# State space part of a hybrid decoder layer: packed array tiles for its tables and its output, shared PSUM banks, one table load

## The chip, the cores and the metric

The kernel runs on one core of one Trainium2 chip. The core has a matmul engine (PE, TensorE), a vector engine (DVE), a scalar engine (ACT) and a general engine (POOL), each with a queue of its own that it works off in order; SP issues most DMAs. Matmuls write to PSUM, eight banks of 512 f32 columns by 128 partitions; everything else lies in SBUF or in DRAM. The metric is the time of one execution in microseconds, as the device measures it. The time before is 2601.95 us, the median of three runs.

## The reference

One layer for one sequence of 2048 tokens, width 1024. Its input projection feeds two groups: forgetting attention with 8 heads of 64, and a state space group with 32 groups of 16 channels and 64 complex states each. Both outputs are normalised and go through one output projection; a gated MLP with a short convolution follows. The change touches the state space group alone:

```python
def s5_ssm(u, a_re, a_im, log_dt, b_re, b_im, c_re, c_im, d_skip, w_glu, b_glu):
    lam = lax.complex(a_re, a_im)
    dt = jnp.exp(log_dt)[:, None]
    lam_bar = jnp.exp(lam * dt)
    b_bar = ((lam_bar - 1.0) / lam)[:, :, None] * b_mat
    bu = jnp.einsum('bsgc,gpc->bsgp', ug, b_bar)
    _, h = lax.associative_scan(_scan_op, (a, bu), axis=1)
    y = jnp.real(jnp.einsum('bsgp,gcp->bsgc', h, c_mat)) + d_skip * ug
    z = jax.nn.gelu(y)
    gate = jnp.einsum('bsgc,gcd->bsgd', z, w_glu) + b_glu
    out = z * jax.nn.sigmoid(gate)
```

## The kernel before, in words

The 2048 tokens are 256 chunks of 8, and the 32 groups are 16 pairs, so that a pair has 2 x 64 states on the 128 partitions, and 2 x (8 x 16) inputs of a chunk. Within a chunk the inputs act on the outputs directly through a block Toeplitz matrix (128 x 128 for each group, `tt_d`); between chunks a state is carried.

`ssm_tables` prepares, in four batches of four pairs, all that depends on the parameters alone, and writes it to DRAM: `tab_d` (for each pair 1024 columns: 256 that bring the inputs into the state, 512 of cosines and sines, 256 that bring the state into the outputs) and `tt_d`. For `tt_d` there are products of 16 x 128 (L785, L786), 64 in all, each of 64 rows; DVE copies them into the tile `kz` (L787) and adds D on the diagonal; eight shifted DMAs for each half (L795) lay `kz` out as the Toeplitz matrix. `wb` (L800 to L802) is the transposed input table.

`ssm` then runs over the 16 pairs. `stage_a` of pair p loads the tables, transposes the inputs (`in_ps`, L838), forms the inputs of the state (`ss_ps`, L846: four products of 64 output rows), and on DVE turns them by cosine and sine, scans over the 256 chunks (L857) and turns them back to `hs` (L851 to L864). `stage_b` of pair p - 1 forms y (`y_ps`, L872 to L874: for each group one product with `ttg` and two with `ft`, in which the other group's 64 rows are zero), the GELU with two ACT and two DVE instructions (L877 to L881, result `z`), the gate product (`g_ps`, L886), its tanh (L889), their product on DVE (L892), four transposes (`tr_ps`, L897) and two copies to `vout` (L900). `y_ps` has a bank of its own; `g_ps` and `tr_ps` share a second one by turns; `in_ps` and `ss_ps` share a third. A bank comes free when its last reader is done. The `ft` tiles are zeroed once, and two DMAs a pair fill their halves (L822). After each fourth pair the outputs go to DRAM (L926), and `mix_t` reads them back as `row` (L1194), takes the squares, scales the rows (L1202), transposes them (L1206) and hands them to the output projection (L1232).

The functions record what is to be done; a scheduler interleaves this into one order for each engine, by its own estimate of when each buffer and operand is ready. The state space part is recorded with high priority. What it leaves free is filled by what is recorded behind it and is ready: attention of block 0 (L952 to L1054), and the query, key and value products of blocks 2 and 3 (L470 and L437, 24 matmuls for each result); when these are done, attention of block 1. DVE does the lower halves, sums and maxima of the attention (L956, L959, L1009, L1017) and the vectors `ada_mid` (L1113) in the same queue as the state space part.

The lines of the change stand one to four lower in its own numbering: there the y products are L871 and L875, the gate product L886, the output transposes L894 (all on `y_ps`), the inputs L837 and L845, the query, key and value products L470 and L437 as before, and attention L948 to L1050.

Of the kernel before, what the change touches and what calls it, by code (L numbers as in the profile page):

```python
# [12 lines left out]
F32 = mybir.dt.float32  # L13
# [3 lines left out]
AF = mybir.ActivationFunctionType  # L17
ALU = mybir.AluOpType
AX = mybir.AxisListType
# [3 lines left out]
P = 128  # L23
# [6 lines left out]
NG = 32  # L30
NPAIR = NG // 2
# [89 lines left out]
def hybrid_layer(ctx, tc, x, c_t, w_ada, b_col, gains, w_flat, bf_row, a_re, a_im, log_dt,  # L121
# [526 lines left out]
    def ssm_tables(pp):  # L648
        misc_ps = prep_ps
# [14 lines left out]
        Q.dma_start(ci, sc_im)  # L664
        ds_t = tl("ds", [16, NG])
        Q.dma_start(ds_t, dskip)

# [38 lines left out]
        V.tensor_tensor(out=fi, in0=fi, in1=den, op=ALU.mult)  # L706
        bbr, bbi, t16 = tl("bbr", [P, NPAIR, 16]), tl("bbi", [P, NPAIR, 16]), tl("t16", [P, NPAIR, 16])
        b3 = [P, NPAIR, 16]
# [34 lines left out]
        def batches(marks):  # L743


            kz = tl("kz", [16, 4, 16, 16])
            G.memset(kz[:, :, 0:8, :], 0.0)
            kt = kz[:, :, 8:16, :]
            for q in range(4):
                with tc.issue_after(marks[q].ins):  # L750
# [28 lines left out]

                    for half in range(2):  # L780
                        ps = misc_ps()
                        rs = slice(half * 64, half * 64 + 64)
                        for pr in range(4):
                            po = ps[0:16, pr * P : (pr + 1) * P]
                            T.matmul(po, lhsT=bbr[rs, 4 * q + pr, :], rhs=f_re[rs, pr, 0:8, :], start=True, stop=False)  # L785
                            T.matmul(po, lhsT=bbi[rs, 4 * q + pr, :], rhs=f_im[rs, pr, 0:8, :], start=False, stop=True)  # L786
                        V.tensor_copy(kt, ps[0:16, :].rearrange("c (g m d) -> c g m d", g=4, m=8))  # L787
                        dg = tl("dg", [16, 4, 16])
                        dsq = ds_t.rearrange("c (q p h) -> c q h p", q=4, h=2)[:, q, half, :]
                        V.tensor_tensor(out=dg, in0=ident[0:16, 0:16].unsqueeze(1).broadcast_to([16, 4, 16]),  # L790
                                        in1=dsq.unsqueeze(2).broadcast_to([16, 4, 16]), op=ALU.mult)
                        V.tensor_tensor(out=kt[:, :, 0, :], in0=kt[:, :, 0, :], in1=dg, op=ALU.add)
                        dst = tt_d[q].rearrange("(p h) k n -> h k p n", h=2)[half]
                        for j in range(8):
                            Q.dma_start(dst[j * 16 : (j + 1) * 16], kz[:, :, 8 - j : 16 - j, :].rearrange("c g m d -> c g (m d)"))  # L795
                    for pr in range(4):
                        wb = tl("wb", [P, 2 * P])
                        ps = misc_ps()
# [11 lines left out]
    def ssm(sp, sps):  # L810

        fts = [sp.tile([P, 2, 2, P], F32, name=f"ft{i}", bufs=1) for i in range(2)]
        for ft in fts:
            G.memset(ft, 0.0)
# [52 lines left out]
        def stage_b(p, vout, ft, ttg, glt, ug, hs):  # L867

            yp = sps.tile([P, 512], F32, name="y_ps", tag="y", bufs=1)
            for g in range(2):  # L870
                yo = yp[:, g * 256 : (g + 1) * 256]  # L871
                T.matmul(yo, lhsT=ttg[:, g, :], rhs=ug[:, g, :], start=True, stop=False)  # L872
                T.matmul(yo, lhsT=ft[:, 0, g], rhs=hs[:, 0, 0:256], start=False, stop=False)
                T.matmul(yo, lhsT=ft[:, 1, g], rhs=hs[:, 1, 0:256], start=False, stop=True)  # L874

            y2 = sp.tile([P, 512], F32, name="y2", tag="y2", bufs=1)
            A.activation(y2, yp, AF.Square, scale=math.sqrt(0.044715))  # L877
            V.scalar_tensor_tensor(out=y2, in0=y2, scalar=1.0, in1=yp, op0=ALU.add, op1=ALU.mult)
            A.activation(y2, y2, AF.Tanh, scale=math.sqrt(2.0 / math.pi))
            z = sp.tile([P, 512], F32, name="z", tag="z")  # L880
# [3 lines left out]
            th = sp.tile([P, 512], F32, name="th", tag="th")  # L884
            for g in range(2):
                T.matmul(gp[:, g * 256 : (g + 1) * 256], lhsT=glt[:, g, :], rhs=z[:, g * 256 : (g + 1) * 256],  # L886
                         start=True, stop=True)
            for g in range(2):
                A.activation(th[:, g * 256 : (g + 1) * 256], gp[:, g * 256 : (g + 1) * 256], AF.Tanh, scale=0.25,  # L889
                             bias=hb[:, 2 * p + g : 2 * p + g + 1])  # L890
            o4 = th
            V.scalar_tensor_tensor(out=o4, in0=th, scalar=1.0, in1=z, op0=ALU.add, op1=ALU.mult)  # L892
            c0 = (p % 4) * 32
            pt = sps.tile([P, 512], F32, name="tr_ps", tag="out", bufs=1)  # L894
            for kb in range(2):
                for g in range(2):
                    T.transpose(pt[:, (2 * kb + g) * P : (2 * kb + g + 1) * P],  # L897
                                o4[:, g * 256 + kb * P : g * 256 + (kb + 1) * P], ident)
            for kb in range(2):
                A.activation(vout[kb][:, :, c0 : c0 + 32].rearrange("k t (g c) -> k g t c", g=2),  # L900
                             pt[:, kb * 256 : (kb + 1) * 256].rearrange("k (g t c) -> k g t c", g=2, t=8), AF.Copy, scale=0.25)

# [1024 lines left out]
```

## Time and profile before

| | |
|---|---|
| three runs | 2596.57, 2601.95, 2602.49 us |
| profiled execution | 2602.08 us, of which the span 2600.4 us |
| instructions | 35785 |
| mean granted clock of PE | 0.98 |
| HBM | 374.32 MB read, 139.59 MB written |

The span runs from the first instruction to the last. A busy share is the mean over stages with different limits; the chain of waits tells which engine's work ended last. Matmuls are pipelined, so that one row of PE can begin before the one ahead of it has ended: the distance between two starts is what a matmul costs, not its length. An f32 product is two records of PE. The state space part stands between 348.7 us (first input transpose) and 573.0 us (last output transposes).

### The profile page before, as it was taken

To read this page: it belongs to the slowest core of one execution; us is meant where nothing else is said; L and a number is where in the kernel's file an instruction comes from. 1 tells how busy PE (TensorE), PEld (TensorE's weight loads), DVE (VectorE), ACT (ScalarE), POOL (GpSimd) and SP (SyncE) were. 2 spreads that over 40 slices of the span, in tenths; PEclk is the share of its full clock that TensorE was granted. 3 is DMA by queue.
4 is the path that set the end of the run, shared out by engine and by line. 5 is a ranking of instruction groups with operands and counts; after the bars stand their busy time and mean duration, and the time that the engine had idled before them with its cause. 6 is when DMAs were issued, how large, how long until landed. Compare 5 with 4: busy or idle time off the path is not lost.

```text
span 2600.4 us, 35785 instructions
## 1 busy us (share of the span) xinstructions
PE 2506.6 (96%) x12107; PEld 2046.8 (79%) x12107; DVE 2046.1 (79%) x3952; ACT 1253.3 (48%) x2120; POOL 152.2 (6%) x160
## 2 busy tenths in 40 slices
PE   5999899998999999999999999999989999999997
PEld 3888778887788888888878888888767888887876
DVE  7989688976787878787877777776589888886777
ACT  3423255643464545465655555556554554553213
POOL 0001000000000000000000000000002333320000
PEclk8899999998899999999999999999999999999998
DMA  8577987667456655656557555556733443448573
GB/s 300 171 240 228 287 275 212 205 195 239 165 195 219 197 191 185 196 170 217 189 192 231 183 172 191 177 177 222 242 105 126 173 155 133 158 144 294 195 272 124
DMA packets 269319, 516.36 MB, mean 199 GB/s; under 512 B 27952, under 2 KB 114864, under 8 KB 269136
## 3 DMA queue, kind: packets, MB, share of 16 engines
q1 hardware_dynamic: 267312, 508.84, 59.3%
q0 software_dynamic: 1280, 4.20, 0.4%
q8 instruction: 96, 1.57, 0.3%
q10 hardware_dynamic: 544, 1.05, 0.1%
q14 instruction: 87, 0.71, 0.1%
HBM read 374.32 MB, written 139.59 MB: 198 GB/s over the span
## 4 chain that ended last, share of the span: by engine, by line
PE 81%; DVE 8%; DMA 6%; ACT 2%; issue 2%; SPq 1%; POOL 0%; POOLq 0%; DVEq 0%; ACTq 0%
PE ff_ps L1258 18%; PE ff_ps L1232 7%; PE up_x L1382 7%; PE up_z L1382 4%; PE up_y L1382 4%; PE ff_ps L1290 3%; PE ff_ps L1292 3%; PE ff_ps L1291 3%; PE o_ps L1018 2%; PE o_ps L1022 2%; PE acc_x L1612 2%; PE vq_ps L470 2%; PE qs_ps L470 2%; DMA wada<-in_w_ada 2%; PE proj_ps L437 2%
## 5 line engine op out<-in xcount | busy, mean ns | idle before, releaser
L86 ACT CAST w_hi<-w_raw 128x1024 fp32r<-128x1024 f32 (+4 forms) x187 | 173.2, 927 | 268.6 <-DMA w_raw<-in_w_flat 69.7
L1258 PE MATMUL ff_ps<-h_hi,w_lo 128*128 128x512 f32 x704 | 277.7, 394 | 1.0 <-DMA w_lo<-wlo 1.0
L1258 PE MATMUL ff_ps<-h_hi,w_hi 128*128 128x512 f32 x704 | 277.7, 396 | 0.6 <-ACT h_hi L388 0.4
L1258 PE MATMUL ff_ps<-h_lo,w_hi 128*128 128x512 f32 x704 | 278.1, 395 | 0.0
L87 DVE TENSOR_TENSOR w_lo<-w_raw,w_hi 128x1024 fp32r<-128x1024 f32 (+4 forms) x187 | 199.7, 1068 | 62.4 <-ACT w_hi L86 51.6
L1009 DVE TENSOR_TENSOR pl<-pf,ph 128x512 fp32r<-128x512 f32 (+1 forms) x320 | 194.7, 618 | 19.8 <-ACT ph L1008 18.9
L1008 ACT CAST ph<-pf 128x512 fp32r<-128x512 f32 (+1 forms) x320 | 177.9, 568 | 61.0 <-PE o_ps L1018 57.2
L1017 DVE TENSOR_TENSOR acc<-acc,pf 128x512 f32<-128x512 f32 (+2 forms) x264 | 159.4, 605 | 44.7 <-ACT pf L1007 39.4
L1007 ACT ACTIVATE pf<-sc_ps 128x512 f32<-128x512 f32 (+3 forms) x184 | 96.3, 528 | 128.3 <-PE sc_ps L998 76.1
L1258 PEld LDWEIGHTS ff_ps<-h_hi,w_lo 128*128 128x128 f32 x704 | 133.0, 189 | 29.9 <-DMA w_lo<-wlo 1.4
L1258 PEld LDWEIGHTS ff_ps<-h_hi,w_hi 128*128 128x128 f32 x704 | 132.9, 189 | 29.4 <-DVE h_f L400 0.7
L1258 PEld LDWEIGHTS ff_ps<-h_lo,w_hi 128*128 128x128 f32 x704 | 132.9, 189 | 28.5 <-issue 0.2
L116 ACT CAST w_hi<-w_raw 128x1024 fp32r<-128x1024 f32 (+2 forms) x100 | 96.5, 965 | 110.6 <-PE ff_ps L1258 50.8
L1291 PE MATMUL ff_ps<-act_lo,w_hi 128*128 128x512 f32 x352 | 138.4, 394 | 0.0
L1292 PE MATMUL ff_ps<-act_hi,w_lo 128*128 128x512 f32 x352 | 138.4, 394 | 0.0
L1290 PE MATMUL ff_ps<-act_hi,w_hi 128*128 128x512 f32 x352 | 138.1, 395 | 0.0
L1018 PE MATMUL o_ps<-ph,vv 128*128 128x512 f32 (+1 forms) x320 | 121.0, 379 | 1.2 <-ACT ph L1008 1.2
L1022 PE MATMUL o_ps<-pl,vv 128*128 128x512 f32 (+2 forms) x312 | 117.0, 377 | 2.5 <-DVE pl L1009 2.3
L1382 PE MATMUL up_x<-hh,w_hi 128*128 128x512 f32 x352 | 112.0, 398 | 3.4 <-ACT hh L385 1.9
L1382 PE MATMUL up_z<-hh,w_hi 128*128 128x512 f32 x308 | 97.6, 398 | 2.9 <-ACT w_hi L86 2.9
L86 ACT CAST w_hi<-s 128x1024 fp32r<-128x1024 f32 (+2 forms) x66 | 62.1, 944 | 78.1 <-DVE s L1583 22.1
L437 PE MATMUL proj_ps<-wu_hi,h_hi 128*128 128x264 f32 (+1 forms) x256 | 76.2, 304 | 13.4 <-ACT h_hi L388 11.7
(673 smaller groups left out, 6863.2 us busy)
## 6 DMA issues: line engine op xcount, KB each, us to landing
w_raw<-in_w_flat SPq DMA_DIRECT2D x193, 512.0 KB
w_lo<-wlo SPq DMA_DIRECT2D x68, 512.0 KB
wlo<-w_lo SPq DMA_DIRECT2D x52, 512.0 KB
kb<-kb SPq DMA_DIRECT2D x80, 256.0 KB
vv<-v SPq DMA_DIRECT2D x80, 256.0 KB
w_raw<-in_w_flat SPq DMA_DIRECT2D x40, 384.0 KB
w_raw<-in_w_flat SPq DMA_DIRECT2D x40, 320.0 KB
wada<-in_w_ada SPq DMA_DIRECT2D x48, 256.0 KB
```

Of the source, the lines that this page charges most:

```text
L86: nc.scalar.copy(hi[:, :n], raw[:, :n])
L87: nc.vector.tensor_tensor(out=lo[:, :n], in0=raw[:, :n], in1=hi[:, :n].bitcast(F32), op=ALU.subtract)
L1008: A.copy(ph[:, cs], pf[:, cs])
L1009: V.tensor_tensor(out=pl[:, cs], in0=pf[:, cs], in1=ph[:, cs].bitcast(F32), op=ALU.subtract)
L1018: T.matmul(o_ps[:, cs], lhsT=vt[:, i, :], rhs=ph[:, cs], start=first, stop=False)
L1022: T.matmul(o_ps[:, cs], lhsT=vt[:, i, :], rhs=pl[:, cs], start=False, stop=(b > 0 and ch == b - 1 and i == 3))
L1232: mark[0] = T.matmul(ps, lhsT=lt, rhs=rt, start=(i == 0), stop=(i == 23))
L1258: T.matmul(ps, lhsT=lt, rhs=rt, start=(n == 0), stop=(n == 23))
L1290: T.matmul(ps, lhsT=a, rhs=ah[:, ts], start=(c == 0), stop=False)
L1291: T.matmul(ps, lhsT=a, rhs=al[:, ts], start=False, stop=False)
L1292: mark[0] = T.matmul(ps, lhsT=bb, rhs=ah[:, ts], start=False, stop=(c == n - 1))
L1382: mark[0] = T.matmul(ps, lhsT=lt, rhs=rt, start=(first and n == 0), stop=(n == 11), skip_group_check=not first)
```

## The change

- **Tables.** The Toeplitz products take 32 columns of the array (the next pair's 16 are computed along and not used), and each of the eight products of a batch (4 pairs x 2 groups) has a tile of 64 rows x 32 columns of its own. The two groups go to two banks (`prep_ps` and `misc_ps`). D is added in PSUM by one DVE instruction for each group; ACT copies the result in eight shifted pieces into `kz`, which now holds the Toeplitz form of all four pairs; four DMAs for each group write it. D is loaded by four DMAs.
- **y from the state.** `ft` is part of the one table load and has no zeros: the two products of each group run over its own 64 rows, in the order a = 0 (group 0, group 1), a = 1 (group 0, group 1).
- **Banks.** y, the gate product and the output transposes of a pair share one buffer of two banks, one for each group. y uses columns 0 to 255 of a bank, the gate product 256 to 511, and the transposes again 0 to 255. The buffer comes free for the next pair when `vout` has been copied.
- **Loads.** One DMA of 1024 columns for each pair instead of three, with three buffers instead of two. The zeroing of `ft` goes.

```diff
-            kz = tl("kz", [16, 4, 16, 16])
-            G.memset(kz[:, :, 0:8, :], 0.0)
-            kt = kz[:, :, 8:16, :]
+            kz = tl("kz", [P, 8, 8, 16])
+            for j in range(1, 8):
+                G.memset(kz[:, j, 0:j, :], 0.0)
...
-                    for half in range(2):
-                        ps = misc_ps()
-                        rs = slice(half * 64, half * 64 + 64)
+                    pss = [prep_ps()[:, 0:P], misc_ps()[:, 0:P]]
+                    for n, (w, f) in enumerate(zip(bb, (f_re, f_im))):
                         for pr in range(4):
-                            po = ps[0:16, pr * P : (pr + 1) * P]
-                            T.matmul(po, lhsT=bbr[rs, 4 * q + pr, :], rhs=f_re[rs, pr, 0:8, :], start=True, stop=False)
-                            T.matmul(po, lhsT=bbi[rs, 4 * q + pr, :], rhs=f_im[rs, pr, 0:8, :], start=False, stop=True)
-                        V.tensor_copy(kt, ps[0:16, :].rearrange("c (g m d) -> c g m d", g=4, m=8))
...
+                            for half, ps in enumerate(pss):
+                                rs = slice(half * 64, half * 64 + 64)
+                                T.matmul(ps[32 * pr : 32 * pr + 32], lhsT=w[rs, 4 * q + pr : 4 * q + pr + 2, :],
+                                         rhs=f[rs, pr, 0:8, :], start=(n == 0), stop=(n == 1))
+                    for half, ps in enumerate(pss):
+                        V.scalar_tensor_tensor(out=ps[:, 0:16], in0=idr, scalar=ds_t[:, q, half : half + 1], in1=ps[:, 0:16],
+                                               op0=ALU.mult, op1=ALU.add)
                         for j in range(8):
-                            Q.dma_start(dst[j * 16 : (j + 1) * 16], kz[:, :, 8 - j : 16 - j, :].rearrange("c g m d -> c g (m d)"))
+                            A.copy(kz[:, j, j:8, :], ps[:, 0 : (8 - j) * 16].rearrange("c (m d) -> c m d", d=16))
+                        for pr in range(4):
+                            Q.dma_start(tt_d[q][2 * pr + half].rearrange("(j c) n -> c j n", c=16),
+                                        kz[32 * pr : 32 * pr + 16].rearrange("c j m d -> c j (m d)"))
...
-            tab = sp.tile([P, 768], F32, name="tab", tag="tab")
-            Q.dma_start(tab, tab_d[p // 4][p % 4, :, 0:768])
-            ft = fts[p % 2]
-            for g in range(2):
-                rs = slice(g * 64, g * 64 + 64)
-                Q.dma_start(ft[rs, :, g, :], tab_d[p // 4][p % 4, rs, 768:1024].rearrange("p (a n) -> p a n", a=2))
+            tab = sp.tile([P, 1024], F32, name="tab", tag="tab", bufs=3)
+            Q.dma_start(tab, tab_d[p // 4][p % 4])
+            ft = tab[:, 768:1024].rearrange("p (a n) -> p a n", a=2)
...
-            yp = sps.tile([P, 512], F32, name="y_ps", tag="y", bufs=1)
+            both = sps.tile([P, 2, 512], F32, name="y_ps", tag="y", bufs=1)
+            yp, gp = both[:, :, 0:256], both[:, :, 256:512]
             for g in range(2):
-                yo = yp[:, g * 256 : (g + 1) * 256]
-                T.matmul(yo, lhsT=ttg[:, g, :], rhs=ug[:, g, :], start=True, stop=False)
-                T.matmul(yo, lhsT=ft[:, 0, g], rhs=hs[:, 0, 0:256], start=False, stop=False)
-                T.matmul(yo, lhsT=ft[:, 1, g], rhs=hs[:, 1, 0:256], start=False, stop=True)
+                T.matmul(yp[:, g], lhsT=ttg[:, g, :], rhs=ug[:, g, :], start=True, stop=False)
+            for a in range(2):
+                for g in range(2):
+                    rs = slice(g * 64, (g + 1) * 64)
+                    T.matmul(yp[:, g], lhsT=ft[rs, a], rhs=hs[rs, a, 0:256], start=False, stop=(a == 1))
...
-            gp = sps.tile([P, 512], F32, name="g_ps", tag="out", bufs=1)
...
-            pt = sps.tile([P, 512], F32, name="tr_ps", tag="out", bufs=1)
             for kb in range(2):
                 for g in range(2):
-                    T.transpose(pt[:, (2 * kb + g) * P : (2 * kb + g + 1) * P],
-                                o4[:, g * 256 + kb * P : g * 256 + (kb + 1) * P], ident)
+                    T.transpose(yp[:, kb, g * P : (g + 1) * P], o4[:, g, kb * P : (kb + 1) * P], ident)
```

The scheduler lays out all engines anew, so the order changes far beyond the edited lines. On PE, before, near the end of the state space part (`y_ps` products of pair 15 with the gate product of pair 14 among them, and query products `qs_ps` behind):

```order
L872 MATMUL y_ps<-ug,ttg 128x256
L873 MATMUL y_ps<-hs,ft_3952 128x256
L874 MATMUL y_ps<-hs,ft_3952 128x256
L872 MATMUL y_ps<-ug,ttg 128x256
L886 MATMUL g_ps<-z,glt 128x256 x2
L873 MATMUL y_ps<-hs,ft_3952 128x256
L874 MATMUL y_ps<-hs,ft_3952 128x256
L470 MATMUL qs_ps<-h_lo,w_hi 128x512
```

There y of a pair begins ahead of the gate product of the pair before, and query products follow at once. On PE, in the change, from the output transposes of pair 9 to those of pair 10 (L948 are attention maxima of block 1, L350 and L325 small sums):

```order
L894 MATMUL y_ps<-ident,th 128x128 x4
L350 MATMUL sc_ps<-ones,sq_att 128x1 x4
L325 MATMUL sc_ps<-ones,ada_mid 128x1 x4
L948 MATMUL vq_ps<-ka_3958,qa_3953 128x512
L871 MATMUL y_ps<-ug,ttg 128x256 x2
L875 MATMUL y_ps<-hs,tab 128x256 x4
L845 MATMUL ss_ps<-ug,tab 64x256 x4
L837 MATMUL in_ps<-ident,uc 128x128 x4
L886 MATMUL y_ps<-z,glt 128x256 x2
```

Here y comes behind the output transposes of the pair before, and no query, key or value product is left between the steps; around pairs 14 and 15 there is nothing of another part at all. On DVE, in the change, the same pair 10 (L879 and L882 the GELU, L850 to L860 the next state, L1109 the vectors `ada_mid`):

```order
L879 SCALAR_TENSOR_TENSOR y_4700<-y_4700,y_ps 128x512
L850 TENSOR_TENSOR m_4744<-ss_ps,tab 128x512
L851 TENSOR_TENSOR m_4745<-ss_ps,tab 128x512
L882 SCALAR_TENSOR_TENSOR z<-y_4700,y_ps 128x512
L852 TENSOR_TENSOR m_4744<-m_4744,m_4745 128x256
L853 TENSOR_TENSOR m_4744<-m_4744,m_4745 128x256
L1109 SCALAR_TENSOR_TENSOR ada_mid<-wada,sil,ada_mid 128x512
L856 SCALAR_TENSOR_TENSOR gg<-r_240,m_4744 128x256 x2
L1109 SCALAR_TENSOR_TENSOR ada_mid<-wada,sil,ada_mid 128x512
L859 TENSOR_TENSOR hs<-gg,tab 128x2x256
```

The state of a later pair and the other part's vectors stand behind each of the steps of pair 10, and ahead of the product with its gate.

More of the change, by code (lines that the diff above doesn't have):

```diff
@@ L648, in ssm_tables @@
     def ssm_tables(pp):
-        misc_ps = prep_ps
         sh = [P, NPAIR]
@@ L664, in ssm_tables @@
         Q.dma_start(ci, sc_im)
-        ds_t = tl("ds", [16, NG])
-        Q.dma_start(ds_t, dskip)
+        ds_t = tl("ds", [P, 4, 2])
+        V.memset(ds_t, 0.0)
+        for r in range(4):
+            Q.dma_start(ds_t[32 * r : 32 * r + 16], dskip.rearrange("c (q p h) -> p c q h", q=4, h=2)[r])
         dtt = exp_acc(pp, ld, sh, "ex1")
@@ L706, in ssm_tables @@
         V.tensor_tensor(out=fi, in0=fi, in1=den, op=ALU.mult)
-        bbr, bbi, t16 = tl("bbr", [P, NPAIR, 16]), tl("bbi", [P, NPAIR, 16]), tl("t16", [P, NPAIR, 16])
+        bb = [tl(nm, [P, NPAIR + 1, 16]) for nm in ("bbr", "bbi")]
+        for t in bb:
+            V.memset(t[:, NPAIR], 0.0)
+        bbr, bbi = (t[:, 0:NPAIR] for t in bb)
+        t16 = tl("t16", [P, NPAIR, 16])
         b3 = [P, NPAIR, 16]
@@ L796, in batches @@
                     for pr in range(4):
                         wb = tl("wb", [P, 2 * P])
-                        ps = misc_ps()
+                        ps = prep_ps()
                         for a, e in enumerate((e_re, e_im)):
@@ L879, in stage_b @@
             A.activation(y2, y2, AF.Tanh, scale=math.sqrt(2.0 / math.pi))
[L880 removed]
+            z = sp.tile([P, 2, 256], F32, name="z", tag="z")
             V.scalar_tensor_tensor(out=z, in0=y2, scalar=1.0, in1=yp, op0=ALU.add, op1=ALU.mult)
[L883 to L884 removed]
+            th = sp.tile([P, 2, 256], F32, name="th", tag="th")
             for g in range(2):
[L886 to L887 removed]
+                T.matmul(gp[:, g], lhsT=glt[:, g, :], rhs=z[:, g], start=True, stop=True)
             for g in range(2):
[L889 to L890 removed]
+                A.activation(th[:, g], gp[:, g], AF.Tanh, scale=0.25, bias=hb[:, 2 * p + g : 2 * p + g + 1])
             o4 = th
```

15 lines of the change are left out of this document (4 added, 11 removed).

## The prediction

> **What bounds the kernel now.** I read the page's busy times and its chain of waits first, then the windows, then the timeline of single engines.
>
> ```profile
> PE 2506.6 (96%) x12107; PEld 2046.8 (79%) x12107; DVE 2046.1 (79%) x3952; ACT 1253.3 (48%) x2120; POOL 152.2 (6%) x160
> ...
> PE 81%; DVE 8%; DMA 6%; ACT 2%; issue 2%; SPq 1%; POOL 0%; POOLq 0%; DVEq 0%; ACTq 0%
> ```
>
> PE carries 81% of the chain that ends last, so matmul time removed in a stretch where PE never waits comes off the end, and idle PE time is added to it. Four windows cut the span at marks of the state space part: its first input transpose (348.7), the output transpose of pair 0 (390.3) and of pair 15 (573.0), and the first product of the output projection (624.2).
>
> ```profile
> 348.70:390.30 41.60, 36.93 (x184) 28.38 (x184) 39.73 (x86) 22.77 (x45) 0.20 (x1) 0.96 0.82 255
> 390.30:573.00 182.70, 182.70 (x1048) 151.44 (x1047) 158.03 (x329) 102.42 (x217) 1.54 (x6) 1.00 0.67 199
> 573.00:624.20 51.20, 44.11 (x306) 39.48 (x305) 32.03 (x81) 23.61 (x47) 0.20 (x1) 0.92 0.88 286
> 624.20:2600.40 1976.20, 1936.69 (x8684) 1567.65 (x8682) 1536.37 (x2691) 989.84 (x1585) 130.10 (x106) 0.99 0.55 186
> ```
>
> After the length come busy PE, PEld, DVE, ACT and POOL, the granted clock, and DMA. Between pairs 0 and 15 PE is busy all 182.7 us although each pair is a long chain over PE, ACT and DVE: query, key and value products (L437, L470) of other blocks stand between its steps. DVE is the second limit, as two windows of 10 us show:
>
> ```profile
> 370.00:380.00 10.00, 7.17 (x31) 4.97 (x31) 9.97 (x21) 5.59 (x10) 0.00 (x0) 0.85 0.94 276
> ...
> 490.00:500.00 10.00, 10.00 (x70) 8.83 (x69) 9.95 (x25) 5.85 (x16) 0.00 (x0) 1.00 0.57 159
> ```
>
> With enough other matmuls (490) both engines are full; without (370), a full DVE leaves PE at 7.17 and the clock at 0.85.
>
> **The matmul work.** PE's timeline (start, length, line):
>
> ```profile
> 403.26 1.08 PE L846 MATMUL ss_ps<-ug,tab 128*64 128x256 f32 x8
> 404.27 0.44 PE L997 MATMUL sc_ps<-qb,kb 128*128 128x384 f32 x1
> ...
> 408.73 0.59 PE L886 MATMUL g_ps<-z,glt 128*128 128x256 f32 x2
> 409.16 0.59 PE L873 MATMUL y_ps<-hs,ft 128*128 128x256 f32 x2
> ...
> 256.90 0.39 PE L785 MATMUL prep_ps<-tb_f_re,tb_bbr 64*16 64x128 f32 x2
> 257.13 0.38 PE L786 MATMUL prep_ps<-tb_f_im,tb_bbi 64*16 64x128 f32 x2
> ```
>
> An f32 product is two records, and a full one of 256 columns holds PE for 409.16 - 408.73 = 0.43 us. Four of them would take 1.73. The four of ss_ps, which use halves of the array's columns, take 404.27 - 403.26 = 1.01: with the order A A B B of the two halves, each second record overlaps the next tile's first. The change gives the four state products of y halves of the rows in the same order. No run shows row halves. Bounds: nothing gained, or 0.86 by perfect overlap. I take ss_ps's 1.01, its nearest row: 16 x (1.73 - 1.01) = **-11.5 us** (0 to -13.9), all in stretches where PE is full.
>
> The trace has one switch into smaller tiles per pair and shows no gap behind it. The Trainium skill (TensorEngine Tiling (Array Packing), Tiling Modes, Key Properties) says that changing the mode drains the engine. By that rule 32 more switches, at the 0.16 us by which the 0.59 rows' second halves outlast their slot, would add an estimated 5 us to the sum below; the row after ss_ps does not bear it out.
>
> The tables' products take 257.13 - 256.90 = 0.22 each, 64 of them 14 us. On eight different tiles they should take some 9 half slots for 16: -6. DVE loses eight copies of 0.67 us, ACT gains 64 small copies (about 0.2 each, 13 us) into a kz buffer that must first be read out by the DMAs of the previous half. SP issues 32 table writes for 64, three more loads of D near the start, and one more 512 KB table ahead of the first vin. In that part PE, DVE and DMA wait for one another, so I take **-3** (-6 to +8). The removed ft loads (two issues a pair) and the two memsets are off the path: nothing, for SP's queue is 1% of the chain.
>
> **What moves.** The order of PE changes far more than its work. In before, 21 to 39 query, key and value matmuls stand between the output transposes of neighbouring pairs, and 227 are left after pair 15's. In the change it is 48 to 100 up to pair 9, then none, and none is left. The cause is readable in the code: y, gate product and output transposes share one buffer, so y of a pair queues behind the vout copies of the pair before, and the order was laid out with wider gaps for that. In the first nine pairs this is harmless: PE is as full as before. From pair 10 on the cover is gone. What is then late is DVE, whose rows for pairs 9 to 13 have these prices (timeline, and one group):
>
> ```profile
> 391.92 0.69 DVE L851 TENSOR_TENSOR m<-ss_ps,tab 128x512 f32<-128x512 f32 x1 [1.60 <-DMA ttg<-tt]
> 392.52 0.68 DVE L852 TENSOR_TENSOR m<-ss_ps,tab 128x512 f32<-128x512 f32 x1
> 393.24 0.42 DVE L853 TENSOR_TENSOR m<-m,m 128x256 f32<-128x256 f32 x1
> 393.58 0.42 DVE L854 TENSOR_TENSOR m<-m,m 128x256 f32<-128x256 f32 x1
> 393.92 1.26 DVE L857 TENSOR_TENSOR_SCAN gg<-r,m 128x256 f32<-128x256 f32 x2
> ...
> 396.88 0.42 DVE L864 TENSOR_TENSOR hs<-hs,m 128x256 f32<-128x256 f32 x1
> ...
> L1113 DVE SCALAR_TENSOR_TENSOR ada_mid<-wada,sil,ada_mid 128x512 f32<-128x512 f32 x10 | 7.5, 751 | 6.0 <-DMA wada<-in_w_ada 5.9
> ```
>
> Starts follow at 0.60 for 512 columns and 0.34 for 256; the state half of a pair takes 391.92 to 397.3 = 5.4 us, and three 512-wide products make it 7.2. Five pairs: 36. Between them the order places 30 other 512-wide rows (17), 29 narrower (10.5), 2 of 1024 columns (2), 8 ada_mid (5.5) and some 30 small ones (3): 38. Together 74 us, in order, while PE has 44 us of work there. Pairs 14 and 15 stand bare on both engines. Their chain is read from one pair of before:
>
> ```profile
> 555.23 0.84 ACT L889 ACTIVATE th<-g_ps,hb 128x256 f32<-128x256 f32 x2 [0.87 <-PE g_ps L886]
> 556.10 0.60 ACT L877 ACTIVATE y<-y_ps 128x512 f32<-128x512 f32 x1
> 557.45 0.63 ACT L879 ACTIVATE y<-y 128x512 f32<-128x512 f32 x1 [0.76 <-DVE y L878]
> ...
> 561.50 0.66 ACT L900 ACTIVATE vout<-tr_ps 128x256 f32<-128x256 f32 x2 [1.99 <-PE tr_ps L897]
> ```
>
> 1.87 (y) + 0.60 + 0.68 + 0.63 + 0.68 + 0.86 (gate) + 0.84 + 0.68 + 0.43 (transposes) + 0.66, and about 0.9 for ten hand-overs: 9 us a pair, 18 for two. So pairs 9 to 15 take 74 + 18 = 92 us. PE's work there is 22 for the seven y, gate and transpose sets, 7 for five state halves, 20 for 150 other matmuls: 49. Idle PE: **+43** (22, if DVE gets half of its other rows done in advance, to 61, if it waits a fifth of the time as well).
>
> Behind pair 15 its rows go to memory and come back before the output projection. The chain of waits of before:
>
> ```profile
> 573.21 0.45 PE tr_ps L897 x4
> ...
> 583.68 5.58 DMA row<-ssm
> ...
> 594.56 1.67 DVE row L1202 x4
> ...
> 623.74 0.48 PE ff_ps L356
> ```
>
> 573.2 to 596 is the way out and back; the rest to 624 waits for attention, which the change has finished by then. The change's way: 23, 2 less for the shorter queue on SP, 5 more because eight attention rows of DVE (0.6 each) are placed inside the norm, 4 for the first scaled rows: 30. PE has 43 matmuls there where before it had 285, mostly of the two kinds of these rows:
>
> ```profile
> 187.13 5.59 PE vq_ps L470 x24
> ...
> 329.13 2.88 PE vq_ps L437 x24
> ```
>
> At 0.23 and 0.12 each (others by their columns; so were the 20 us above) that is about 7 us for 36 of the 51.2. So 23 uncovered for 15: **+8** (-5 to +20).
>
> The attention matmuls placed in the gaps are missing later: neutral, as PE is 98% busy from 624 on.
>
> **Sum**, against the profiled execution's own 2602.08 (span 2600.4 and 1.7 around it; the median of three runs is 2601.95, 0.1 lower): -11.5 - 3 + 43 + 8 = +36.5, so **2638.6 us**.
>
> **Rivals.**
> 1. *The gaps cost nothing* (not slower). DVE does its other rows of pairs 9 to 13 early, so that a pair needs no more than PE's 9 us instead of 14, and the way out of pair 15 stays covered. It decides at 44 us for those five pairs. For it: PE was full with DVE full at 490. Against: DVE's order is fixed, and the window at 370. Then 2602.1 - 14.5 = 2588. 10%.
> 2. *Idle PE is made up later.* The span from 624 has 39.5 us of idle PE; if attention that is already done shortens half of it and the tail is at its lower end, -14.5 + 20 + 8 - 15 gives about 2601. Against: these waits stand at the norms and at the very end. 10%.
> 3. *The row halves do not overlap* (the change doesn't do what it says): +11.5, 2650. For it: no row shows them; against: ss_ps. 12%.
> 4. *ACT's copies hold up the projections* in the tables' part, waiting for the previous half's DMAs as the wb copies do today: +8 for -3, 2650. 8%.
> The forecast's own case has 60%.
>
> **How the numbers follow.** The forecast with its term bounds spans about 2610 to 2660; 3 and 4 push up; 2 lies below. 2604 to 2664 leaves out rival 1, part of 2 and the far ends. A measurement of this kernel tells about 0.3% (7.8 us) from no change: slower by more, 0.82 (forecast, 3 and 4, and a little of 2); within, 0.08; faster, 0.10.
>
> **What would show it.** In the profile of the change: y from the state as groups of eight records in about 1.01 us; PE full up to about pair 9, then windows with DVE near full and PE at half, lower granted clock with it; some 92 us from pair 8's transposes to pair 15's; about 30 us from there to the output projection, which starts near 670 rather than 624, and less than 1976 us from it to the end (about 18 less, the matmuls done ahead). Wrong would be: the last pairs 10 us apart or less, or the same distance from the projection to the end.

## The result and the profile after

| | before | after |
|---|---|---|
| median, of 5 runs each | 2602.49 us (2596.57 to 2605.57) | 2682.31 us (2681.06 to 2684.89) |
| ratio, 95% interval | | 1.031 (1.029 to 1.032) |
| span of the profiled execution | 2600.4 us | 2679.9 us |
| mean granted clock of PE | 0.98 | 0.96 |

One run of e7 below, the one that was traced, took 7151 us for 2676 to 2681 in its other three; it is left out, and no trace of e7 is used.

The change costs 80 us. From the page of after: the busy times (the engine, us, share of the span), PE's busy tenths and granted clock by slices of 67 us, and the shares of the chain of waits:

```profile
PE 2521.8 (94%) x12107; PEld 2045.6 (76%) x12107; DVE 2044.2 (76%) x3940; ACT 1266.1 (47%) x2184; POOL 149.9 (6%) x164
...
PE   6897989997599999999999999999989999999997
...
PEclk8898999997699999999999999999999999999998
...
PE 77%; DVE 10%; DMA 8%; ACT 2%; issue 2%; SPq 1%; POOL 0%; POOLq 0%; ACTq 0%; DVEq 0%
```

PE's idle time grew from 2600.4 - 2506.6 = 94 us to 158, so by 64 of the 80. Its busy time grew by 15 as well, though its work shrank: the clock fell with the idle time, visible in the tenth and eleventh slice (7 and 6 tenths). The same windows as before, cut at the first input transpose (366.9), the output transposes of pairs 0 (409.9), 8 (583.9) and 15 (700.2) and the output projection (734.2); length, PE, PEld, DVE, ACT, POOL, clock, DMA share and GB/s:

```profile
366.90:409.90 43.00, 38.66 (x191) 29.09 (x190) 38.85 (x81) 23.31 (x47) 0.21 (x1) 0.96 0.78 239
409.90:583.90 174.00, 172.90 (x1052) 142.08 (x1051) 135.18 (x282) 92.95 (x187) 1.23 (x6) 1.00 0.71 215
583.90:700.20 116.30, 83.17 (x364) 57.97 (x362) 75.24 (x163) 41.13 (x88) 2.49 (x6) 0.73 0.38 118
700.20:734.20 34.00, 15.98 (x55) 11.28 (x56) 15.90 (x54) 12.94 (x27) 0.00 (x0) 0.58 0.44 128
734.20:2679.90 1945.70, 1907.05 (x8569) 1546.88 (x8567) 1501.56 (x2608) 974.36 (x1552) 127.88 (x101) 0.99 0.55 187
```

The state part starts 18 us later. From pair 0 to pair 15 it takes 290 us for 183: full to pair 8, then 116 us with PE at 83 and the clock at 0.73. The output projection starts 110 us later, and what follows is 30.5 us shorter. In the chain of after, two places: a pair in the full stretch, then the last pair and the way out (start, length, engine, tile, line, count):

```profile
414.53 0.86 PE y_ps L871 x4
415.39 1.06 PE y_ps L875 x8
416.45 1.12 PE qs_ps L470 x4
...
689.56 2.07 PE y_ps L871 x4
691.63 2.03 PE y_ps L875 x8
693.75 0.61 ACT y L878
...
696.50 2.09 PE y_ps L886 x4
...
700.23 1.13 PE y_ps L894 x4
701.38 0.67 ACT vout L896 x2
...
709.91 6.64 DMA row<-ssm
```

At full clock the eight records of the row halves (L875) take 1.06 us; in the last pair the same records take twice as long, at half clock.

### The profile page after: what moved, and what is told of

Its sections match the earlier page's. It is cut to its first block, busy times and chain, and to the rows that moved or that the text cites. A ratio compares the mean times of both kernels' runs of the same rounds, so it can differ in the third digit from the quotient of the medians.

```text
span 2679.9 us, 35740 instructions
## 1 busy us (share of the span) xinstructions
PE 2521.8 (94%) x12107; PEld 2045.6 (76%) x12107; DVE 2044.2 (76%) x3940; ACT 1266.1 (47%) x2184; POOL 149.9 (6%) x164
## 4 chain that ended last, share of the span: by engine, by line
PE 77%; DVE 10%; DMA 8%; ACT 2%; issue 2%; SPq 1%; POOL 0%; POOLq 0%; ACTq 0%; DVEq 0%
PE ff_ps L1254 18%; PE ff_ps L1228 7%; PE up_x L1378 6%; PE up_z L1378 4%; PE up_y L1378 4%; PE ff_ps L1286 3%; PE ff_ps L1287 3%; PE ff_ps L1288 3%; PE o_ps L1014 2%; PE o_ps L1018 2%; PE qs_ps L470 2%; DMA wada<-in_w_ada 2%; PE vq_ps L470 2%; PE acc_x L1608 2%; PE sc_ps L993 1%
```

## The experiments

Medians and intervals against the kernel before, run on the same chip in between. The other columns come from the trace: start of the state part, time from pair 0's to pair 15's output transposes, from there to the output projection, and from the projection to the end (us).

| kernel | median | ratio | start | pairs | way out | rest |
|---|---|---|---|---|---|---|
| before | 2602.5 | | 349 | 183 | 51 | 1976 |
| after | 2682.3 | 1.029 to 1.032 | 367 | 290 | 34 | 1946 |
| e1_tables_only | 2621.6 | 1.007 to 1.012 | 364 | 188 | 52 | 1980 |
| e2_state_only | 2677.9 | 1.028 to 1.031 | 351 | 290 | 34 | 1961 |
| e3_shared_banks | 2666.9 | 1.024 to 1.027 | 346 | 287 | 34 | 1954 |
| e4_gate_apart | 2658.9 | 1.021 to 1.024 | 351 | 282 | 34 | 1954 |
| e5_two_wb | 2623.4 | 1.005 to 1.011 | 364 | 187 | 53 | 1981 |
| e6_spread | 2667.1 | 1.024 to 1.028 | 344 | 273 | 28 | 1985 |
| e7_spread_apart | 2678.4 | 1.027 to 1.033 | | | | |
| e8_spread_whole | 2698.4 | 1.036 to 1.040 | 363 | 281 | 28 | 1984 |
| e9_one_qkv_bank | 2658.1 | 1.021 to 1.024 | 350 | 160 | 123 | 1987 |
| e10_four_banks | 2649.7 | 1.018 to 1.021 | 348 | 165 | 107 | 1990 |
| e11_tables_dve | 2623.0 | 1.008 to 1.010 | 365 | 184 | 56 | 1978 |
| e12_tables_one_bank | 2615.2 | 1.005 to 1.008 | 354 | 189 | 51 | 1979 |
| e13_norm_first | 2614.1 | 1.004 to 1.007 | 348 | 179 | 62 | 1977 |
| e14_four_banks_late | 2610.3 | 1.003 to 1.006 | 345 | 165 | 74 | 1986 |
| e15_change_one_bank | 2673.7 | 1.026 to 1.031 | 355 | 278 | 35 | 1961 |
| e16_tables_repaired | 2620.6 | 1.006 to 1.010 | 358 | 180 | 61 | 1983 |
| e17_all_repaired | 2629.2 | 1.009 to 1.013 | 353 | 161 | 79 | 1990 |
| e18_spread_inside | 2641.6 | 1.014 to 1.018 | 347 | 246 | 33 | 1972 |

### Which part, and which edit of it (e1 to e4)

e1 takes the tables' hunks of the diff alone, e2 those of the state part alone. e3 and e4 cut e2 further:

```diff
 e3: e2 with the full-array products and the loads of before
-T.matmul(yp[:, g], lhsT=ft[rs, a], rhs=hs[rs, a, 0:256], ...)
+T.matmul(yp[:, g], lhsT=ft[:, a, g], rhs=hs[:, a, 0:256], ...)
 e4: e2 with gate and transposes in the bank of in_ps
-yp, gp = both[:, :, 0:256], both[:, :, 256:512]
+yp = both[:, :, 0:256]
+gp = sps.tile([P, 2, 256], F32, name="g_ps", tag="in", bufs=1)
+pt = sps.tile([P, 2, 256], F32, name="tr_ps", tag="in", bufs=1)
```

> The kernel before with the tables' part of the change alone (array tiles, the bank of misc_ps beside prep_ps, ACT's kz copies, eight table DMAs per batch); the state part is that of before. Theory A (the tables' part costs what its stage shows: the trace of the change starts the state part 18.2 us later than before, and no one makes it up): about 2602 + 18 = 2620 us, first transposes of uc near 367. Rival B (the late start is only projections and attention placed earlier, since the state part of the change asks for PE otherwise; the tables' part itself is free, as I had predicted with -3): within 8 us of 2602, first transposes of uc near 347.

> The change with the tables' part of before (state part alone: row tiles, two shared banks, one table load). Theory A (the two parts add): 2682 - 18 = 2664 us, state part from 349, 333 us from its start to pair 15's transposes. Rival B (the tables' part costs nothing): 2682. Rival C (the state part alone would be as good as its 11.5 us of PE less, and only the late and uncovered start of the change breaks it): at or below 2602.

> The kernel before with one edit of the state part alone: y, gate and transposes share one buffer of two banks, as in the change; y's products from the state stay full arrays with the zeroed tables of before, with its three loads. Theory A (the shared buffer holds pair p+1's y products back until pair p's last copy, so that the order puts twice the filler between pairs and none is left for pairs 10 to 15): as state_only plus what the row halves save, 2664 + 11 = 2675 us, pairs 12 us apart at the end with PE at half. Rival B (the row halves or the load are what costs): at 2602 within 8 us.

> As state_only (tables of before, row tiles into two banks, one load), but gate and transposes no longer stand in y's banks: they take turns with in_ps and ss_ps in the third bank, so that y's banks are free after z. Theory A (it is y's buffer held to the end of a pair that stretches a pair): faster than state_only by 40 or more, about 2602 to 2620. Rival B (any two steps of a pair that share a bank stretch it alike; before had a bank for each): within 10 us of state_only, about 2660, with no projections between the last pairs either.

e1 gave theory A: the tables' part costs 21 us, not -3. e2 costs 77, nearer to its rival B than to A: the losses of 21 and 77 do not add up to 80. Up to the output projection they nearly do (+18 and +95 for +110); the difference lies in the rest, 1946 in after against 1961 in e2, with the same matmuls left. Of these 15 us PE is busy 9 less and idle 6 less; what sets the rest apart stays open. e3 gave theory A in kind: the shared buffer by itself costs 66. The row halves with the single load, which save PE time, make e2 11 slower than e3 (the intervals do not touch), where A had them 11 faster; why is open too. e4 lies between its theories: 19 us better than e2, with pairs that still take 282. Sharing the bank of in_ps instead costs nearly as much.

### Order or buffer (e6, e7, e8, e18)

In e2's trace 63 to 96 projection products stand between neighbouring pairs up to pair 8, 24 between pairs 8 and 9, and none after that, much as in after. To test the order alone, the projections of batches 2 and 3 were cut into their 32 pieces and each held behind a pair: in e6, e7 and e8 behind its output transposes, in e18 behind its y products.

```diff
+HOLD = {2: [None, None, 0, 1, 2, 3, ...], 3: [10, 11, 12, 12, 13, ...]}   (e18; another list in e6 to e8)
+def behind_pair(b, n):
+    p = HOLD.get(b, [None] * 16)[n]
+    return ExitStack() if p is None else tc.issue_after(done[p].ins)
...
-qk(ms)
+with behind_pair(b, ms[0]):
+    qk(ms)
...   (e18)
-T.matmul(yp[:, g], lhsT=ft[rs, a], ..., stop=(a == 1))
+done[p] = T.matmul(yp[:, g], lhsT=ft[rs, a], ..., stop=(a == 1))
```

> As e2_state_only (2677.9 us), but the projections of batches 2 and 3 may not start all at once: in 32 pieces, each held behind the output transposes of a pair (from pair 0 to pair 15), so that PE's order has 24 to 48 projection products between neighbouring pairs, as before had, and some 190 behind pair 15. Nothing else changes. Theory A (the cover theory: only the order spends the filler too early; a pair by itself needs no more than before's 12 us): pairs 12 to 14 apart, output projection near 625 to 640, 2590 to 2612 us. Rival B (the shared buffer makes a pair's own chain some 16 to 20 us long, whatever stands between): PE idles in every pair, pairs stay 17 or more apart, the output projection starts near 700 and the time is 2650 or more.

> The same spread projections as e6_spread, on the variant with gate and transposes in the bank of in_ps (e4_gate_apart, 2658.9 us). Theory A (order alone): within 10 us of e6_spread. Rival B (the shared buffer's own chain): faster than e6_spread by 20 us or more, if y's banks are what makes a pair long; as slow as it, if any shared bank does.

> The whole change (2682.3 us) with both repairs: spread projections and two wb buffers. Theory A (order in the state part, one wb buffer in the tables' part): both losses gone and the row halves' 11 us kept, 2588 to 2605 us. Rival B (the pair's own chain): 2650 or more. If only one of the repairs works, near 2620 (tables not repaired) or 2665 (state part not repaired).

> As e6_spread, but each held piece of the projections comes behind a pair's y products instead of its output transposes. In e6 the 24 products of a piece stood right ahead of the next pair's y (4.3 us from the vout copies to y on average), so they lengthened the pair's chain instead of lying beside it; here they lie between y and the gate, where the shared buffer makes PE wait anyway. Theory A (only the place and the spending of the cover, not the buffer): pairs 12 to 13.5 apart, 2595 to 2615 us. Rival B (the buffer's chain alone: in e6 y to gate 9.2, gate to transposes 4.5, transposes to the copies' end 1.6, together 15.3 us without any lump): pairs 15 to 16.5 apart, PE idle 2 to 3 us in each, output projection 640 to 665, 2630 to 2655 us.

e6 stayed at 2667, with 53 us of idle PE between the start of the state part and pair 15; e7 was 11 slower than e6, and e8, with the tables' part, 16 slower than the unrepaired change. But in e6 the held piece stood ahead of the next y and so in the chain of a pair, which makes it no fair test of the order. e18 is a fairer one: 2641.6, 36 better than e2, and short of theory A's 2615 by 27. Its pairs and its time are as B had them. Two pairs of e18 in the timeline (start, length, engine, line, operation, tiles):

```profile
419.11 0.66 PE L897 MATMUL y_ps<-ident,th 128*128 128x128 f32 x4 [0.59 <-DVE th L893]
420.48 0.67 ACT L899 ACTIVATE vout<-y_ps 128x256 f32<-128x256 f32 x2
421.20 1.13 PE L874 MATMUL y_ps<-ug,ttg 128*128 128x256 f32 x4 [0.16 <-ACT vout L899]
422.26 1.13 PE L878 MATMUL y_ps<-hs,tab 64*128 64x256 f32 x8
423.44 0.60 ACT L881 ACTIVATE y<-y_ps 128x512 f32<-128x512 f32 x1 [0.49 <-PE y_ps L878]
...
425.45 0.69 DVE L885 SCALAR_TENSOR_TENSOR z<-y,y_ps 128x512 f32<-128x512 f32 x1 [0.70 <-ACT y L883]
428.70 1.02 PE L889 MATMUL y_ps<-z,glt 128*128 128x256 f32 x4
...
433.49 0.60 PE L897 MATMUL y_ps<-ident,th 128*128 128x128 f32 x4
```

The copies of one pair's transposes end at 421.15, and the next pair's y begins at 421.20. So each pair runs through alone. From pair 1 to 15, on the mean, it takes 9.2 us from y to the gate, 4.9 to the transposes, 2.0 to the end of the copies and 0.2 more to the next y: 16.3. In before the same steps are longer, 12.6, 6.8 and 1.6, but the next pair's y begins 8.8 us *before* the copies end, so that pairs are 12.2 apart. In e18 too the held piece lies partly in the chain: above, z is done at 426.14 and its gate product begins at 428.70, and on the mean of pairs 1 to 15 PE is busy with other work for 3.3 us between the two. PE's waits in e18 from 380 to 640 us (total, times, longest) name the chain:

```profile
PE y_ps L897 <- DVE th L893: 16.7, 8, 4.2
PE y_ps L874 <- ACT vout L899: 4.1, 7, 0.8
```

Of the state part's 77 us, then, 35 go when only the order changes (77 and 42, each against its own runs of before). The other 42 stay with the buffer, the row halves and the single load in this order; that no order with the shared buffer does better is not shown.

### Nothing shared (e9, e10, e14)

A fourth bank separates everything, and the projections must give it up. e9 is the control: before, with one bank for the projections of batches 2 and 3. e10 adds the state part with y in two banks, gate and transposes in the third, in_ps in the fourth. In e14 only batch 2 has one bank; batch 3 gets the second when the state part is done.

```diff
 e9, e10
-qs_last_ps = opened(att_ctx, "qs_last", ...)
-qs_ps = pair_ps(qs_last_ps)
+qs_ps = vq_ps
...
 attention((0,))
+qs_last_ps = opened(att_ctx, "qs_last", ...)
 e10: e4 with tag="out" for g_ps and tr_ps
 e14: e10 with
+return vq_ps() if n < 16 or n % 2 else qs_last()
```

> The kernel before, in which the projections of batches 2 and 3 use one bank (vq) instead of two while the state part runs; the second is opened behind it, for attention's later use. It is the control for e10_four_banks. No theory of the change hangs on it: a group of 24 products must now wait for the copies of the group before, so 2600 to 2630 us, with pairs still 11 to 14 us apart.

> e9_one_qkv_bank with the state part of the change, but with nothing shared: y in two banks of its own for the row halves, gate and transposes in their own bank as before, in_ps and ss_ps in theirs (four banks instead of three; the fourth is the one that e9 gives up); one table load. Theory A (sharing y's banks with gate and transposes makes a pair's own chain some 17 us long; the row halves themselves gain 0.67 us per pair): pairs 11 to 14 apart, the output projection within 15 us of e9's, and 5 to 12 us faster than e9. Rival B (the row halves or the single table load are what makes a pair long): pairs 17 or more apart, 40 us or more slower than e9.

> As e10_four_banks (2649.7 us; nothing shared, row halves, one table load), but only batch 2's projections use a single bank; batch 3's, most of which stand behind pair 15, use two again, the second opened when the state part is done. Theory A (e9 and e10 lost their 50 us there: between pair 15 and the output projection PE waits 25 us and runs at a lower clock): 30 to 55 us faster than e10, 2592 to 2620; below 2600 if the row halves' 8 to 11 us are all that is left. Rival B (the single bank costs during the pairs too): 2630 or more.

With nothing shared the pairs overlap again: 165 us in e10 and 160 in e9, where e2 had 290. So neither the row halves nor the single load is what makes a pair long. Against its control e10 is 8.5 us faster, with row halves, one load and a second bank for y; their intervals do not touch. That is within theory A's 5 to 12. The output projection starts 20 us earlier than in e9, more than A's 15, and the rest is 3 longer, so that not all of the difference can be traced to the row halves. The one bank itself cost e9 more than its expectation allowed, behind pair 15. Windows from there to the output projection, e9 and then e14:

```profile
551.00:674.00 123.00, 90.21 (x372) 70.81 (x371) 50.97 (x106) 36.42 (x63) 2.28 (x5) 0.79 0.55 167
```

```profile
546.20:620.00 73.80, 65.85 (x359) 56.63 (x357) 43.20 (x90) 30.90 (x52) 1.56 (x3) 0.95 0.79 249
```

e9 waits there after each group of 24 products for the copies that empty the bank, as PE's waits from 545 to 680 us say:

```profile
PE vq_ps L470 <- DVE qk_lo L476: 15.2, 6, 2.9
```

e14 removes that (39 us better than e10) and reaches the projection at 620, ahead of before's 624. It still ends 11 us later than before: matmuls of 20,500 columns (9 us at 0.23 for 512) that before had done by then are left for the rest.

### Where the tables' 21 us are (e5, e11, e12, e13, e15, e16, e17)

PE in the slice from 240 to 260 us, before and then after:

```profile
240.00:260.00 20.00, 20.00 (x138) 17.34 (x137) 18.60 (x35) 7.58 (x17) 2.17 (x3) 1.00 0.67 202
```

```profile
240.00:260.00 20.00, 8.79 (x46) 7.16 (x45) 14.21 (x31) 7.03 (x12) 4.74 (x8) 0.60 0.57 171
```

Among the waits of e1 from 100 to 366 us two named wb's buffer:

```profile
PE prep_ps L806 <- ACT tb_wb L807: 9.3, 3, 4.9
...
ACT tb_wb L807 <- DMA tab<-tb_wb: 24.1, 9, 5.4
```

```diff
 e5: e1 with
-wb = tl("wb", [P, 2 * P])
+wb = tl("wb", [P, 2 * P], bufs=2)
 e11: e1 with
-A.copy(kz[:, j, j:8, :], ...)
+V.tensor_copy(kz[:, j, j:8, :], ...)
 e12: e1 with
-pss = [prep_ps()[:, 0:P], misc_ps()[:, 0:P]]
+for half in range(2):
+    ps = prep_ps()[:, 0:P]
+    ...
 e13: e1 with
-batches(marks + marks[-1:])
 rows0 = load_x(0)
+batches(marks + marks[-1:])
 e15: after with e12's edit   e16: e5, e12 and e13 together   e17: e16 and e14
```

> The tables' part alone (as e1_tables_only, 2621.6 us) with two buffers for wb in place of one, so that a copy no longer waits for the DMA that empties the only one. Theory A (the 20 us are the last batch's four transposes, each held about 5 us by that DMA with nothing between them): most of the 20 comes back, 2602 to 2608, PE over 17 of 20 in the slices from 240 to 260, first transposes of uc near 350. Rival B (the array tiles and ACT's 64 copies are what costs, or two DMAs for one buffer of the shifted columns): at 2621 within 5 us.

> e1_tables_only (2621.6 us) with the 64 copies of the shifted columns on DVE in place of ACT. Theory A (the rival that I gave 8% in the prediction: on ACT these copies wait for the DMAs that empty their one buffer, 5 us at a time, and w_hi, qk_hi, ust and h_hi behind them wait too, so that the projections are held up): 8 us or more of the 20 come back, 2600 to 2614. Rival B (where they stand does not matter; the tables' rows now stand earlier in every engine's order, ahead of the projections' rows, and the projections are late for it): 2615 to 2635, as before or worse for DVE's 13 us more.

> e1_tables_only (2621.6 us) with one edit: the two halves of a batch's products go through prep_ps's bank one after the other, as before, instead of one of them through misc_ps's bank; array tiles, ACT's copies and DMAs stay. Theory A (misc_ps is also the bank of the norms' sums: the norm of batch 0, which comes behind the tables in the program, waits for their last product, its sums at 238.7 us where before had them at 144.1, and u's projection of batch 0 and all that hides the tables' waits comes late): the norm is back near 140 to 175, 2595 to 2608 us. Rival B (the tables' rows themselves, wherever they write): 2615 to 2630.

> e1_tables_only with another single edit: the load and norm of batch 0 are written ahead of the tables' batches instead of behind them, so that the norm gets misc_ps first; the tables keep both banks. Theory A (the norm's place behind the tables in a shared bank): 2595 to 2610. Rival B (the tables' rows themselves): 2615 to 2630.

> The whole change (2682.3 us) with e12's edit: the tables' halves through prep_ps's bank alone. Theory A (two independent losses): the first transposes of uc return to about 348, the state part keeps its own loss, so as e2_state_only: 2665 to 2680. Rival B (the tables' late start is made up anyway in the whole change, as e2's 2677.9 against its 2682.3 suggests): no difference beyond 4 us from 2682.

> The tables' part alone with three repairs at once: batch 0's norm written ahead of the tables, the halves through prep_ps's bank alone, and two wb buffers (e1 2621.6, with the norm first 2614.1, with one bank 2615.2). Theory A (the norm behind a shared bank is the first loss and the transposes behind the one wb buffer the second, which showed in e12 with 9.2 us of waits and could gain nothing in e5 as long as the norm was late): 2598 to 2608. Rival B (what is left after the norm is the array products and the copies behind them): 2612 to 2618, as e13.

> e16's tables' part with e14's state part (four banks, row halves, one table load): all repairs of the whole change. Theory A (the parts add): 2610.3 + (e16 - 2599), so 2608 to 2620, no better than before. Rival B (the state part now gains its row halves' 11 us, since the tables no longer start it late): 2590 to 2600.

Neither the second wb buffer (e5) nor the copies on DVE (e11) gave anything back. The bank did look like the cause. PE's timeline has the sums of batch 0's norm, in before and then in e1:

```profile
144.06 0.28 PE L350 MATMUL misc_ps<-ones,sq_acc 128*128 128x1 f32 x2
```

```profile
238.70 0.95 PE L350 MATMUL misc_ps<-ones,sq_acc 128*128 128x1 f32 x8
```

The tables of the change take misc_ps's bank, in which the norms' sums stand, and the norm of batch 0 comes 95 us later. Both ways of undoing that bring the sums back (148 us in e12, 138 in e13) and are 6 and 8 us faster than e1, where theory A wanted 12 or more; the intervals of all three overlap. With everything together (e16) it was 2620.6, no better than e1, although its sums stand at 153. So theory A fails, and the 6 to 8 us of e12 and e13 are not shown to be the norm's, nor to be there at all. What these seven kernels with the new tables share (e1, e5, e11, e12, e13, e16, e17) is 57 to 69 us of idle PE ahead of the state part for 43 in before, and the surplus moves: in e1 most of it lies between 200 and 260 us, in e12 between 90 and 120 and between 210 and 240. What puts it there stays open. e15 (2673.7) cannot be told from after by its interval, and e17 shows that all repairs together (2629.2) remain behind before, and behind both of its theories. No version beat the kernel before.

## Why the prediction was right or wrong

- **Direction right, size too small:** 2638.6 (2604 to 2664) forecast, 2682.3 measured. (The bounds of its terms, all added, reach from 2599 to 2691; its range was narrower.) The marks in the trace give the parts: start of the state part +21 us over the forecast, start to pair 8 +15 (217 measured; its marks of 670, 92 and 30 leave 202), pairs 9 to 15 +24, way out +4, and the rest -12 (30.5 shorter where 18 was expected); together 52, of which 9 are what the prediction's marks lack to its own sum.
- **By PE's time the failed steps are two: the tables' wait, and the slower clock, which was priced at nothing.** The span grew by 79.5 us. Idle PE gives 64: 20 ahead of the state part (63 for 43), 34 from the start of the state part to pair 15, 11 on the way out, -1 behind. Busy PE gives 15, where the forecast had -11.5 and, for the tables' products, -6. The mean clock of 0.980 and 0.962 means 104 and 204 us of the two spans at half clock; in the traces PE is busy in 76 and 137 of these. Work takes about twice as long there, as the eight records do (2.03 for 1.06), so the 61 us more cost an estimated 30, and some -15 are left for the work itself. The idle time of the state part, then, was forecast well (43 + 8 = 51 for 45). What the sum lacked is 20 us of waits in the tables' part and the 30 of the clock: the prediction expected "lower granted clock with it", but all its prices are those of the full clock.
- **Row halves, -11.5: right in kind, some 2 us too large.** The eight records take 1.06 us where 1.01 was taken, so rival 3 fell. The Trainium skill (TensorEngine Tiling (Array Packing), Tiling Modes, Key Properties) says that a change of mode drains the engine; the prediction saw no gap and gave it nothing. There is one, on both sides of the group (PE's timeline of after):

```profile
414.36 1.02 PE L871 MATMUL y_ps<-ug,ttg 128*128 128x256 f32 x4
415.32 1.13 PE L875 MATMUL y_ps<-hs,tab 64*128 64x256 f32 x8
416.38 0.50 PE L470 MATMUL qs_ps<-h_hi,w_lo 128*128 128x512 f32 x1
```

  The four full records hold PE for 0.96 us, where four take 2 x 0.43 = 0.86 without a change behind them; the eight take 1.06, where full overlap would give 0.86. That is 0.30 us a pair, near the 0.32 that I had estimated by the rule and left out of the sum; that the drain is its cause is not shown apart from the weight loads. The gain is 1.73 + 0.86 - 1.06 - 0.96 = 0.57 a pair, 9.1 for 16. In the end time it shows in e10 against e9 (8.5 us, with the load and y's second bank), not in e2 against e3, where it is lost for a reason that stays open.
- **Tables' part, -3 (-6 to +8): wrong, and outside its bounds.** e1 measured +21. The prediction summed matmul prices and saw PE, DVE and DMA "wait for one another", and then priced no wait; what causes the wait stays open. Rival 4, ACT's copies, found no support either (e11).
- **"In the first nine pairs this is harmless: PE is as full as before": true of PE's idle time, not of the cover.** PE is full there (172.9 of 174.0), but with work that before still had behind pair 15: nine pairs took 217 us instead of 134. Ahead of the output projection the trace of after has only 76 products of 512 columns more than before (18 us at 0.23), and it takes 92 us more from the first input transpose to the projection. Of the other 74, 45 are PE idle later on, and most of the remainder is its work at half clock.
- **Pairs 9 to 15, 92 us: measured 116.** I took DVE's rows in order as the limit. But DVE was busy only 75 of the 116. PE's waits point to the pair's own chain, alternately on PE, ACT and DVE, for z and th; one wait of 6.9 us for m came on top of it. How much of each was a DVE row of another part standing ahead is not shown. PE's waits in after from 583.9 to 734.2 us:

```profile
PE sc_ps L948 <- DMA kx<-kb: 15.6, 1, 15.6
PE in_ps L837 <- DVE m L851: 7.6, 2, 6.9
PE y_ps L894 <- DVE th L890: 7.2, 5, 1.8
PE y_ps L886 <- DVE z L882: 7.1, 4, 2.9
```

  The two bare pairs took 12.0 and 12.5 instead of 9, since the PE steps of the chain (y, gate, transposes) run at half clock; in the last pair 2.07 + 2.03 + 2.09 + 1.13 = 7.3 us where I took 1.87 + 0.86 + 0.43 = 3.2.
- **Way out, 30 us: measured 34.** PE idles 18 us there, mostly the 15.6 above, for 7.1 in before: +11 for a term of +8, so right in size. The long wait is for the load of kx, an operand of attention.
- **Rest, 18 shorter: 30.5.** The work done ahead was sized right (18 us). e2, with the same work done ahead, is 16 shorter. PE's idle time here is 39.5 us in before, 38.7 in after and 44.7 in e2; PE is busy at half clock for 34, 20 and 36 us, which is an estimated 7 of the other 12 in after. Why its clock was higher here stays open. Rivals 1 and 2 fell: the idle time was neither free nor made up.

## What to carry to other kernels

Before two stages of a pipeline are put in one buffer, write down from which instruction to which each stage holds it: the next item starts only when the last holder has let go, and the time between items becomes the whole chain. A forecast of such a change should start with that chain, by items, and treat filler that runs in its gaps as borrowed from where it stood before. A part that only "costs a few copies" in a stage where three engines wait for one another is worth a trace of its own before it gets a small number. And where a forecast expects idle PE, its matmuls have to be priced at the clock that goes with it.

## What was not expected of the hardware

The granted clock falls to half, and stays there, in stretches without a long pause. In the slice from 680 to 700 us of after PE is busy 10.51 of 20, and its waits there, for z and th, are at most 2.9 us long (the rows above); from 684.3 on the clock is at half throughout:

```profile
680.00:700.00 20.00, 10.51 (x32) 5.99 (x30) 3.96 (x6) 4.79 (x10) 0.00 (x0) 0.59 0.00 0
684.30:700.20 15.90, 9.01 (x24) 5.09 (x23) 2.76 (x4) 3.56 (x8) 0.00 (x0) 0.50 0.00 1
```

The Trainium skill (TensorE: Matmul & The Clock Gate, HAM oscillation — how this bites in real kernels) puts the limit at idle gaps above about 3.4 us. Here a pair has pauses of 2.9, 1.7 and 0.8 us, and from 655.3 to 700.2 us PE has none above 2.9. So a gap of that length was not needed; which measure of idle time decides is not shown.
